# The 64-row score products of two heads (or two maps) by turns into two PSUM banks, in a fixed order on TensorE

## The chip, the cores and the metric

One Trainium2 chip, of which the kernel uses one core. Each engine of the core (TensorE, VectorE, ScalarE, GpSimd, SyncE) takes its instructions in the order in which they stand in the built program, and semaphores tie the engines together. The metric is the device time in microseconds (us) of the whole launch.

## The reference

Three transformer-like blocks one after another on x of 512 tokens by 1024 channels, all in float32. The change touches score products in the first two blocks. Each contracts over 64 channels:

```python
# block 1: 4 heads, 2 maps each, 64 channels per map
sc = jnp.einsum("bhmqd,bhmkd->bhmqk", qb, kt)          # per block of 128 queries
p = jax.nn.softmax(jnp.where(mask, sc, -jnp.inf), axis=-1)
a = p[:, :, 0] - lam * p[:, :, 1]
...
# block 2, gated delta rule: 8 heads of 64 channels
lower = jnp.where(strict, jnp.einsum('bhncd,bhnsd->bhncs', k_beta, k) * decay, 0.0)
attn = jnp.where(causal, jnp.einsum('bhncd,bhnsd->bhncs', q, k) * decay, 0.0)
...
# block 2, rwkv7: 8 heads of 64 channels, token by token
sa = jnp.einsum('bhvk,bhk->bhv', S, a_t)
S = S * w_t[:, :, None, :] + sa[..., None] * b_t[:, :, None, :] + v_t[..., None] * k_t[:, :, None, :]
y_t = jnp.einsum('bhvk,bhk->bhv', S, r_t)
```

The kernel computes both recurrences in chunks of 128 tokens, so that rwkv7 too has score products: of b and k with a (strictly lower part) and of b and k with r.

## The kernel before

The kernel is written in a tile language: the program text says what is computed, tile pools give out buffers, and a scheduler decides when building it in which order each engine's instructions stand. `z.first()` raises the priority of what is inside. What sets the order is therefore text order, priority and the scheduler's own idea of when operands and buffers are ready.

Activations lie with channels on the 128 partitions and 512 tokens along the free side. Two heads, or the two maps of one head, of 64 channels each share a tile: the first on partitions 0 to 63, the second on 64 to 127. A score product of one of them is a matmul with 64 rows (partitions) of contraction; the profile writes it 64\*128. A float32 matmul appears in the trace as two passes, each a weight load and a MATMUL row.

The big projections (`lin`, tiles `mm`, lines L368 to L370) split weights and activations into high and low parts and use three matmuls of 512 columns for each block of 128 channels. Weights come in pieces of eight blocks: a DMA into `wr`, ScalarE makes `wh` (L324), VectorE makes `wl` (L325); each of these has three buffers. Projections that nothing waits for at the moment stand between the small matmuls and fill TensorE.

Block 1, `first`, loop over 4 heads `hd` and 4 query blocks `i`. For each map `m`: a bank of the pool `sc` (two banks) gets the causal mask by a full-array bf16 matmul (L1005, `neg` with the identity `idb`), the diagonal 128 columns of scores on top (L1006, 64 rows), and the `i` earlier blocks of keys (L1008, 64 rows, 128 to 384 columns). Then VectorE takes the row maximum (L1010) and ScalarE the exponential (L1012); the two maps are normalised and combined on VectorE (L1015 to L1018), transposed on TensorE (L1021, `tp`) and multiplied with v (L1025). Elsewhere in VectorE's order stand the 120 taps of a convolution (L750, tiles `cv`).

Block 2, `second`, loop over 4 pairs of heads `j`: `rwkv` (tiles `ra`, `fr`, banks `r`, of which there are three) and `gdn` (tiles `ga`, `fg`, banks `g`, two) run as two interleaved generators, next to the projections of pair `j + 1`. In `rwkv` the helper `scores` makes one head's product: four matmuls of 64 rows by 128 columns into one bank (L1370), then a masked product on VectorE (L1372) that frees the bank. It is called for both heads in turn: `bt` with `at`, `kt` with `at`, and near the end `bt` and `kt` with `rt` (`rb`, `rk`). In `gdn` each head has four matmuls of k with k (L1478) and four of k with q (L1486), each set into a bank of its own. A chain of four such matmuls is eight MATMUL rows.

Of the kernel before, what the change touches and what calls it, by code (L numbers as in the profile page):

```python
# [17 lines left out]
P = 128  # L18
# [167 lines left out]
class K:  # L186
# [65 lines left out]
    def first(self, n=HP):  # L252

        return self.tc.high_priority(offset=n)

    def run(self, *gens):

# [695 lines left out]
def first(z, h):  # L953
    V, A, T = z.V, z.A, z.T
    mult, add, sub = ALU.mult, ALU.add, ALU.subtract
    with z.phase({"aux": 1, "sc": 2, "tp": 1, "o": 1}, qk=12, d=4, p=24, cv=(2, 4 * S), f=6, a=6):
# [5 lines left out]
        ps = f.bank(2)  # L962
# [5 lines left out]
        neg = z.new([P, P], BF16, tag="neg")  # L968
# [6 lines left out]
        qk = []  # L975
# [20 lines left out]
        for hd in range(4):  # L996
            ops = z.bank("o")
            for i in range(4):
                n = (i + 1) * P
                pt, sums = [], ac.small(2)  # L1000
                for m in range(2):
                    ps = z.bank("sc")
                    ql = qk[hd][64 * m:64 * m + 64, i * P:n]
                    kr = qk[4 + hd][64 * m:64 * m + 64]
                    T.matmul(ps[:, i * P:n], lhsT=idb, rhs=neg, start=True, stop=False)  # L1005
                    T.matmul(ps[:, i * P:n], lhsT=ql, rhs=kr[:, i * P:n], start=False, stop=True)  # L1006
                    if i:
                        T.matmul(ps[:, :i * P], lhsT=ql, rhs=kr[:, :i * P], start=True, stop=True)  # L1008
                    mx = ac.small(1)
                    V.tensor_reduce(mx, ps[:, :n], axis=AX.X, op=ALU.max, negate=True)  # L1010
                    pm = ac.t()
                    A.activation(pm[:, :n], ps[:, :n], AF.Exp, bias=mx, accum_out=sums[:, m:m + 1])  # L1012
                    pt.append(pm)
                rs = ac.small(2)
                V.reciprocal(rs, sums)  # L1015
                V.tensor_scalar(rs[:, 1:2], rs[:, 1:2], lam, None, op0=mult)
                V.tensor_scalar(pt[1][:, :n], pt[1][:, :n], rs[:, 1:2], None, op0=mult)
                V.scalar_tensor_tensor(pt[0][:, :n], pt[0][:, :n], rs[:, 0:1], pt[1][:, :n], op0=mult, op1=sub)  # L1018
                tp = z.bank("tp")
                for b in range(i + 1):  # L1020
                    T.transpose(tp[:, b * P:(b + 1) * P], pt[0][:, b * P:(b + 1) * P], z.ident)  # L1021
                at = ac.t()
                A.activation(at[:, :n], tp[:, :n], AF.Copy)
                for b in range(i + 1):
                    T.matmul(ops[:, i * P:n], lhsT=vt[b][:, hd * P:(hd + 1) * P], rhs=at[:, b * P:(b + 1) * P],  # L1025
                             start=b == 0, stop=b == i)
            r = ac.rstd(ac.sumsq([ops]), P)
            o = z.tile("d")
            V.scalar_tensor_tensor(o, ops, z.q("subln"), r, op0=mult, op1=mult)
            V.tensor_scalar(o, o, 1.0 - (0.8 - 0.6), None, op0=mult)  # L1030
            diff.append(o)
# [17 lines left out]
        sc = [], []  # L1049
# [246 lines left out]
    z.V.tensor_tensor_scan(out, mask[p0:p0 + x.shape[0]], x, 0.0, op0=ALU.mult, op1=ALU.add)  # L1296


def rwkv(z, j, rkv, kk, lo, vz, out):

    V, A, T = z.V, z.A, z.T
# [60 lines left out]
    inc = z.k("incl").unsqueeze(1).to_broadcast([P, 4, P])  # L1362
    stm = z.k("strict").unsqueeze(1).to_broadcast([P, 4, P])

    def scores(e, lh, rh, mask):
        ps = c.bank()
        rows = slice(64 * e, 64 * e + 64)
        for i in range(4):
            n = slice(P * i, P * i + P)
            T.matmul(ps[:, n], lhsT=lh[rows, n], rhs=rh[rows, n], start=True, stop=True)  # L1370
        o = c.t()
        V.tensor_tensor(ch(o), ch(ps), mask, op=mult)  # L1372
        return o

    Tt, Lt = [], []
    for e in range(2):
        Lt.append(scores(e, bt, at, stm))
        yield
    inv = [c.invert(x, Tt) for x in Lt]
    for g_ in inv:  # L1380
        next(g_)
    yield
    vtok = vz.rearrange("p c (x n) -> p c x n", n=64)[:, :, 0:4:3]
    c.transposes(v, vtok)
    ak = [ch(scores(e, kt, at, stm)) for e in range(2)]
    yield
    ps = c.bank()
    for i in range(4):
# [16 lines left out]
    for _, ps, x in c.solve(Tt, R, UW):  # L1405
        A.activation(x, ps, AF.Copy)
    yield
    rb = [ch(scores(e, bt, rt, inc)) for e in range(2)]
    rk = [ch(scores(e, kt, rt, inc)) for e in range(2)]
    yield  # L1410

    Y = c.t()
# [40 lines left out]
def gdn(z, j, qkv, gd, tok, out):  # L1453

    V, A, T = z.V, z.A, z.T
    mult, add, sub = ALU.mult, ALU.add, ALU.subtract
    ch = lambda x: x.rearrange("p (c n) -> p c n", c=4)
    c = Chain(z, "ga", "g")
    q, k, v = qkv
    inc = z.k("incl").unsqueeze(1).to_broadcast([P, 4, P])  # L1460
    egb = c.t()
    by = lambda a, hd: tok[:, :, a + hd:a + hd + 1].to_broadcast([P, 4, 64])
    Tt, at, inv = [], [], []
    for e in range(2):
        hd = 2 * j + e
        rows = slice(64 * e, 64 * e + 64)
        gb = c.t()
        z.nc.gpsimd.dma_start(gb, gd[hd].partition_broadcast(P))
        A.activation(egb[rows], gb[rows], AF.Exp)
        V.tensor_tensor(ch(gb), ch(gb), tok[:, :, hd:hd + 1].to_broadcast([P, 4, P]), op=sub)  # L1470
        V.tensor_scalar(gb, gb, 0.0, None, op0=ALU.min)
        A.activation(gb, gb, AF.Exp)
        V.tensor_tensor(ch(gb), ch(gb), inc, op=mult)
        yield
        ps = c.bank()
        for i in range(4):
            n = slice(P * i, P * i + P)
            T.matmul(ps[:, n], lhsT=k[rows, n], rhs=k[rows, n], start=True, stop=True)  # L1478
        l = c.t()
        for i in range(4):  # L1480
            n = slice(P * i, P * i + P)
            V.scalar_tensor_tensor(l[:, n], ps[:, n], tok[:, i, 32 + hd:33 + hd], gb[:, n], op0=mult, op1=mult)
        ps = c.bank()
        for i in range(4):
            n = slice(P * i, P * i + P)
            T.matmul(ps[:, n], lhsT=k[rows, n], rhs=q[rows, n], start=True, stop=True)  # L1486
        V.tensor_tensor(gb, ps, gb, op=mult)
        at.append(ch(gb))
        inv.append(c.invert(l, Tt))
        next(inv[-1])  # L1490
        yield
    ktok = ch(c.transposes(k))
    R, vtok, ke, _ = c.pair()
    c.transposes(v, vtok)
    V.tensor_tensor(q, q, egb, op=mult)
    for e in range(2):
        o = slice(64 * e, 64 * e + 64)
        V.tensor_tensor(ke[:, :, o], ktok[:, :, o], by(64, 2 * j + e), op=mult)
        V.tensor_tensor(ktok[:, :, o], ktok[:, :, o], by(96, 2 * j + e), op=mult)
    yield  # L1500
    while inv:
        for g_ in list(inv):
            if next(g_, z) is z:
                inv.remove(g_)
        yield
    Tt = [ch(x) for x in Tt]

    UW, _, W, U = c.pair()
    for a, ps, x in c.solve(Tt, R, UW):
        for e in range(2):  # L1510
            o = slice(P * e, P * e + P)
            V.tensor_tensor(x[:, :, o], ps[:, :, o], tok[:, 2 * a:2 * a + 2, 32 + 2 * j + e:33 + 2 * j + e].to_broadcast([P, 2, P]),
                            op=mult)
    yield
    Y = c.t()
    for e in range(2):
        ps = c.bank()
        o, x = slice(64 * e, 64 * e + 64), slice(64 - 64 * e, P - 64 * e)
        for i in range(4):
            T.matmul(ps[:, i * P:i * P + P], lhsT=UW[:, i, P * e:P * e + P], rhs=at[e][:, i], start=True, stop=True)  # L1520
        A.activation(Y[o], ps[o], AF.Copy)
        V.tensor_tensor(q[o, P:], q[o, P:], ps[x, P:], op=add)
    yield
    ps = c.bank()
    for i in range(3):
        T.matmul(ps[:, i * P:i * P + P], lhsT=ktok[:, i], rhs=U(i), start=True, stop=True)
    Sv = c.t()
    V.tensor_tensor(ch(Sv)[:, :3], ch(ps)[:, :3], z.bd64.unsqueeze(1).to_broadcast([P, 3, P]), op=mult)
    ps = c.bank()
    for i in range(1, 3):  # L1530
        T.matmul(ps[:, i * P:i * P + P], lhsT=W[:, i], rhs=ktok[:, i], start=True, stop=True)
    Kb = c.t()
    V.tensor_tensor(ch(Kb)[:, 1:3], ch(ps)[:, 1:3], z.bd64.unsqueeze(1).to_broadcast([P, 2, P]), op=mult)
    yield
    for i in (1, 2):
        n, b = slice(i * P, i * P + P), slice(i * P - P, i * P)
        ps = c.bank(P)
        T.matmul(ps, lhsT=Kb[:, n], rhs=Sv[:, b], start=True, stop=True)
        V.scalar_tensor_tensor(Sv[:, n], Sv[:, b], egb[:, i * P + 127:i * P + 128], Sv[:, n], op0=mult, op1=add)
        V.tensor_tensor(Sv[:, n], Sv[:, n], ps, op=add)  # L1540
        yield
    ps = c.bank()
    for i in range(1, 4):
        n = slice(i * P, i * P + P)
        T.matmul(ps[:, n], lhsT=Sv[:, n.start - P:n.start], rhs=q[:, n], start=True, stop=True)
    V.tensor_tensor(Y[:, P:], Y[:, P:], ps[:, P:], op=add)
    yield
    out.append((Y,))
# [570 lines left out]
```

## Time and profile before

| | |
|---|---|
| median of 3 runs | 3328.61 us (3328.02 to 3330.11) |
| the profiled execution's own time | 3330.9 us |
| its span, first to last instruction | 3329.1 us |
| TensorE busy (MATMUL) | 3242.3 us, 97% |
| VectorE busy | 2234.4 us, 67% |
| ScalarE busy | 1497.2 us, 45% |
| mean granted TensorE clock | 0.992 |

A MATMUL row lasts longer than the time after which the next one may start, so that rows overlap and busy time says little about what a matmul costs. What it costs is the time from its start to the start of the next row.

### The profile page before, as it was taken

To read this page: it belongs to the slowest core of one execution; us is meant where nothing else is said; L and a number is where in the kernel's file an instruction comes from. 1 tells how busy PE (TensorE), PEld (TensorE's weight loads), DVE (VectorE), ACT (ScalarE), POOL (GpSimd) and SP (SyncE) were. 2 spreads that over 40 slices of the span, in tenths; PEclk is the share of its full clock that TensorE was granted. 3 is DMA by queue.
4 is the path that set the end of the run, shared out by engine and by line. 5 is a ranking of instruction groups with operands and counts; after the bars stand their busy time and mean duration, and the time that the engine had idled before them with its cause. 6 is when DMAs were issued, how large, how long until landed. Compare 5 with 4: busy or idle time off the path is not lost.

```text
span 3329.1 us, 48326 instructions
## 1 busy us (share of the span) xinstructions
PE 3242.3 (97%) x19041; PEld 2700.3 (81%) x19041; DVE 2234.4 (67%) x3675; ACT 1497.2 (45%) x2491; POOL 101.0 (3%) x186
## 2 busy tenths in 40 slices
PE   7999999999999999999999999999999999999998
PEld 6778888888887887887888887888877778888887
DVE  5696645986578577566887567777687996363344
ACT  6443433432346656654332334645546665232222
POOL 0000000000000000000000000000000001000000
PEclk9999999999999999999999999999999999999999
DMA  4223333665332112125367324222227567423332
GB/s 134 64 70 98 95 117 102 215 202 161 107 103 76 46 50 73 58 64 171 122 203 242 95 81 133 69 78 92 81 80 239 171 208 239 131 88 101 95 95 76
DMA packets 128324, 393.33 MB, mean 118 GB/s; under 512 B 16056, under 2 KB 23480, under 8 KB 128096
## 3 DMA queue, kind: packets, MB, share of 16 engines
q1 hardware_dynamic: 113776, 346.82, 33.6%
q0 software_dynamic: 13168, 42.36, 3.7%
q8 instruction: 150, 2.46, 0.3%
q10 hardware_dynamic: 1152, 1.05, 0.1%
q14 instruction: 78, 0.64, 0.1%
HBM read 358.44 MB, written 31.74 MB: 117 GB/s over the span
## 4 chain that ended last, share of the span: by engine, by line
PE 88%; DVE 6%; ACT 4%; issue 2%; DMA 1%; SPq 0%; POOL 0%; DVEq 0%; ACTq 0%; POOLq 0%
PE mm L368 20%; PE mm L369 20%; PE mm L370 20%; PE mm L354 3%; PE mm L355 3%; PE mm L356 3%; PE s L2082 1%; DVE wl L325 1%; PE s L2068 1%; ACT wh L324 1%; PE r L1370 1%; PE g L655 1%; PE mm L405 1%; PE r L655 1%; PE mm L406 1%
## 5 line engine op out<-in xcount | busy, mean ns | idle before, releaser
L368 PE MATMUL mm<-h,wh 128*128 128x512 f32 x2400 | 947.6, 395 | 1.8 <-ACT t L948 1.5
L369 PE MATMUL mm<-h,wh 128*128 128x512 f32 x2400 | 948.5, 395 | 0.0
L370 PE MATMUL mm<-h,wl 128*128 128x512 f32 x2400 | 947.3, 395 | 0.0
L324 ACT ACTIVATE wh<-wr 128x1024 fp32r<-128x1024 f32 x464 | 491.4, 1061 | 949.8 <-PE mm L369 663.5
L325 DVE TENSOR_TENSOR wl<-wr,wh 128x1024 fp32r<-128x1024 f32 x464 | 567.2, 1224 | 467.6 <-ACT wh L324 462.2
L368 PEld LDWEIGHTS mm<-h,wh 128*128 128x128 f32 x2400 | 452.7, 189 | 98.4 <-issue 5.5
L370 PEld LDWEIGHTS mm<-h,wl 128*128 128x128 f32 x2400 | 452.7, 189 | 96.9 <-issue 6.0
L369 PEld LDWEIGHTS mm<-h,wh 128*128 128x128 f32 x2400 | 452.8, 189 | 96.2 <-issue 5.4
L368 PE MATMUL mm<-p,wh 128*128 128x512 f32 x599 | 233.6, 390 | 0.0
L369 PE MATMUL mm<-p,wh 128*128 128x512 f32 x599 | 233.4, 390 | 0.1
L370 PE MATMUL mm<-p,wl 128*128 128x512 f32 x599 | 233.1, 389 | 0.0
L354 PE MATMUL mm<-h,wh 128*128 128x256 f32 (+1 forms) x480 | 159.5, 344 | 14.4 <-DVE t L1930 5.3
L355 PE MATMUL mm<-h,wh 128*128 128x256 f32 (+1 forms) x480 | 160.1, 339 | 1.1 <-DVE h L569 1.0
L356 PE MATMUL mm<-h,wl 128*128 128x256 f32 (+1 forms) x480 | 158.6, 335 | 0.0
L301 DVE SCALAR_TENSOR_TENSOR ac<-wa,adas,ac 128x1024 f32<-128x1024 f32 x98 | 125.5, 1282 | 23.9 <-DMA wa<-wa 23.5
L369 PEld LDWEIGHTS mm<-p,wh 128*128 128x128 f32 x599 | 112.4, 188 | 23.9 <-DVE p L430 0.8
L368 PEld LDWEIGHTS mm<-p,wh 128*128 128x128 f32 x599 | 112.4, 188 | 23.5
L370 PEld LDWEIGHTS mm<-p,wl 128*128 128x128 f32 x599 | 112.4, 188 | 23.4
L354 PEld LDWEIGHTS mm<-h,wh 128*128 128x128 f32 x480 | 92.4, 198 | 25.8 <-ACT h L568 4.6
L355 PEld LDWEIGHTS mm<-h,wh 128*128 128x128 f32 x480 | 94.3, 198 | 10.0 <-DVE h L569 2.0
L356 PEld LDWEIGHTS mm<-h,wl 128*128 128x128 f32 x480 | 94.6, 198 | 8.5
L750 DVE SCALAR_TENSOR_TENSOR f<-mm,par,f 128x511 f32<-128x511 f32 (+1 forms) x128 | 95.5, 746 | 1.1
(661 smaller groups left out, 5244.6 us busy)
## 6 DMA issues: line engine op xcount, KB each, us to landing
wr<-w SPq DMA_DIRECT2D x464, 512.0 KB, 3.7
wa<-wa SPq DMA_DIRECT2D x96, 512.0 KB, 4.3
e<-cum SPq DMA_DIRECT2D x64, 256.0 KB, 5.1
x<-x POOLq DMA_DIRECT2D x40, 256.0 KB, 4.5
s<-ecum SPq DMA_DIRECT2D x64, 128.0 KB, 4.8
cd<-t POOLq DMA_DIRECT2D x24, 256.0 KB, 2.3
gt<-t POOLq DMA_DIRECT2D x16, 256.0 KB, 2.5
fr<-gt SPq DMA_DIRECT2D x16, 256.0 KB, 3.0
```

Source lines behind the costliest of these rows:

```text
L301: self.V.scalar_tensor_tensor(a, raw, s[:, k, m:m + 1], a, op0=ALU.mult, op1=ALU.add)
L324: self.A.activation(hi, raw, AF.Copy)
L325: self.V.tensor_tensor(lo, raw, hi.bitcast(F32), op=ALU.subtract)
L354: self.T.matmul(ps[:, n], lhsT=wh, rhs=x[0][k][:, n], start=k == 0, stop=False)
L355: self.T.matmul(ps[:, n], lhsT=wh, rhs=x[1][k][:, n], start=False, stop=False)
L356: self.T.matmul(ps[:, n], lhsT=wl, rhs=x[0][k][:, n], start=False, stop=k == last)
L368: self.T.matmul(out, lhsT=wh, rhs=x[0][k], start=k == 0, stop=False)
L369: self.T.matmul(out, lhsT=wh, rhs=x[1][k], start=False, stop=False)
L370: self.T.matmul(out, lhsT=wl, rhs=x[0][k], start=False, stop=k == last)
L405: self.T.matmul(ps, lhsT=a, rhs=wl, start=False, stop=False)
L655: self.z.T.transpose(ps[:, c * P:(c + 1) * P], src[:, c * P:(c + 1) * P], self.z.ident)
L750: z.V.scalar_tensor_tensor(out[:, d:], src[:, :S - d], w[:, n - 1 - d:n - d], out[:, d:], op0=ALU.mult, op1=ALU.add)
```

## The change

The two heads (or maps) get their two banks together, and their matmuls are issued by turns, the second one (partitions 64 to 127) first. `in_order` makes the scheduler keep TensorE's order inside as written; other matmuls may still stand in between. In `gdn` the k with k products of both heads now come after the decay tiles of both heads, then the k with q products of both, then both inversions start. In block 1 the two mask matmuls come first, then the diagonals by turns, then the earlier keys by turns; maxima and exponentials of both maps follow.

```diff
+    def in_order(self):
+        return self.tc.manual_schedule(engines={mybir.EngineType.PE})
...
-                for m in range(2):
-                    ps = z.bank("sc")
-                    ql = qk[hd][64 * m:64 * m + 64, i * P:n]
-                    kr = qk[4 + hd][64 * m:64 * m + 64]
-                    T.matmul(ps[:, i * P:n], lhsT=idb, rhs=neg, start=True, stop=False)
-                    T.matmul(ps[:, i * P:n], lhsT=ql, rhs=kr[:, i * P:n], start=False, stop=True)
-                    if i:
-                        T.matmul(ps[:, :i * P], lhsT=ql, rhs=kr[:, :i * P], start=True, stop=True)
+                two = [z.bank("sc") for _ in range(2)]
+                row = [slice(64 * m, 64 * m + 64) for m in range(2)]
+                q_, k_ = qk[hd], qk[4 + hd]
+                turns = [(row[m], two[m]) for m in (1, 0)]
+                with z.in_order():
+                    for _, ps in turns:
+                        T.matmul(ps[:, i * P:n], lhsT=idb, rhs=neg, start=True, stop=False)
+                    for m, ps in turns:
+                        T.matmul(ps[:, i * P:n], lhsT=q_[m, i * P:n], rhs=k_[m, i * P:n], start=False, stop=True)
+                    for m, ps in turns if i else ():
+                        T.matmul(ps[:, :i * P], lhsT=q_[m, i * P:n], rhs=k_[m, :i * P], start=True, stop=True)
+                for m, ps in enumerate(two):
...
+def halves(z, c, lh, rh):
+    two = [c.bank() for _ in range(2)]
+    with z.in_order():
+        for i in range(4):
+            n = slice(P * i, P * i + P)
+            for e in (1, 0):
+                rows = slice(64 * e, 64 * e + 64)
+                z.T.matmul(two[e][:, n], lhsT=lh[rows, n], rhs=rh[rows, n], start=True, stop=True)
+    return two
...
-    def scores(e, lh, rh, mask):
-        ps = c.bank()
-        rows = slice(64 * e, 64 * e + 64)
-        for i in range(4):
-            n = slice(P * i, P * i + P)
-            T.matmul(ps[:, n], lhsT=lh[rows, n], rhs=rh[rows, n], start=True, stop=True)
-        o = c.t()
-        V.tensor_tensor(ch(o), ch(ps), mask, op=mult)
-        return o
+    def scores(lh, rh, mask):
+        out = []
+        for ps in halves(z, c, lh, rh):
+            o = c.t()
+            V.tensor_tensor(ch(o), ch(ps), mask, op=mult)
+            out.append(o)
+        return out
...
-    rb = [ch(scores(e, bt, rt, inc)) for e in range(2)]
-    rk = [ch(scores(e, kt, rt, inc)) for e in range(2)]
+    rb = [ch(x) for x in scores(bt, rt, inc)]
+    rk = [ch(x) for x in scores(kt, rt, inc)]
...
+        at.append(gb)
         yield
-        ps = c.bank()
-        for i in range(4):
-            n = slice(P * i, P * i + P)
-            T.matmul(ps[:, n], lhsT=k[rows, n], rhs=k[rows, n], start=True, stop=True)
+    for e, ps in enumerate(halves(z, c, k, k)):
         l = c.t()
...
-        ps = c.bank()
-        for i in range(4):
-            n = slice(P * i, P * i + P)
-            T.matmul(ps[:, n], lhsT=k[rows, n], rhs=q[rows, n], start=True, stop=True)
-        V.tensor_tensor(gb, ps, gb, op=mult)
-        at.append(ch(gb))
         inv.append(c.invert(l, Tt))
-        next(inv[-1])
-        yield
+    yield
+    for e, ps in enumerate(halves(z, c, k, q)):
+        V.tensor_tensor(at[e], ps, at[e], op=mult)
+        at[e] = ch(at[e])
+    for g_ in inv:
+        next(g_)
+    yield
```

How this moves TensorE's order shows at three places. A row is one instruction of the built program (a float32 matmul is one row here and two in the trace), `x4` stands for four alike, and the number behind a name is the buffer's. First, block 1, second head, last query block, before; `sc265` and `sc268` are the banks of the two maps:

```order
L1005 MATMUL sc265_1186<-neg82_313,idb83_315 128x128
L1006 MATMUL sc265_1186<-qk139_626,qk102_448 128x128
L1008 MATMUL sc265_1186<-qk139_626,qk102_448 128x384
L369 MATMUL mm396_1724<-h23_119,wh390_1632 128x512
L370 MATMUL mm396_1724<-h22_118,wl391_1633 128x512
L368 MATMUL mm396_1724<-h24_120,wh390_1632 128x512
L1005 LDWEIGHTS idb83_315
L1005 MATMUL sc268_1194<-neg82_313,idb83_315 128x128
L1006 MATMUL sc268_1194<-qk139_626,qk102_448 128x128
L1008 MATMUL sc268_1194<-qk139_626,qk102_448 128x384
```

The same place of TensorE's order in the changed kernel (its line numbers are larger by a few: L1011, L1013 and L1015 are L1005, L1006 and L1008 of before, and L372 to L374 are L368 to L370); of the seven projection rows after the first mask matmul the last three are shown:

```order
L1011 MATMUL sc266_1208<-neg82_313,idb83_315 128x128
...
L372 MATMUL mm392_1741<-h30_126,wh386_1649 128x512
L373 MATMUL mm392_1741<-h31_127,wh386_1649 128x512
L374 MATMUL mm392_1741<-h30_126,wl387_1650 128x512
L1011 LDWEIGHTS idb83_315
L1011 MATMUL sc265_1207<-neg82_313,idb83_315 128x128
L1013 MATMUL sc266_1208<-qk139_626,qk102_448 128x128
L1013 MATMUL sc265_1207<-qk139_626,qk102_448 128x128
L1015 MATMUL sc266_1208<-qk139_626,qk102_448 128x384
L1015 MATMUL sc265_1207<-qk139_626,qk102_448 128x384
```

The first mask matmul stands some projections ahead, and the four 64-row matmuls of the two maps stand next to each other, one map after the other. Second, block 2, first pair of heads, TensorE's order at `rb` and `rk` before (two heads of `rb`, then two of `rk`, and the first use of them at L1418):

```order
L1370 MATMUL r1658_8960<-fr1417_7999,ra1470_8280 128x128 x4
L1370 MATMUL r1660_8967<-fr1417_7999,ra1470_8280 128x128 x4
L1370 MATMUL r1662_8974<-fr1417_7999,fr1422_8033 128x128 x4
L1370 MATMUL r1664_8981<-fr1417_7999,fr1422_8033 128x128 x4
L1418 MATMUL r1667_8989<-ra1659_8965,cra1654_8942 128x128
```

And after, from the last two rows of `rb` on (L1315 is the line of `halves`, L1559 is L1545 of before, a product of `gdn`, and L1435 is L1418 of before):

```order
L1315 MATMUL r1658_9016<-fr1417_8047,ra1470_8328 128x128
L1315 MATMUL r1657_9015<-fr1417_8047,ra1470_8328 128x128
L1315 MATMUL r1662_9033<-fr1417_8047,fr1422_8081 128x128
L1559 MATMUL g1665_9049<-fg1432_8149,ga1649_8987 128x128 x3
L1315 MATMUL r1661_9032<-fr1417_8047,fr1422_8081 128x128
L1315 MATMUL r1662_9033<-fr1417_8047,fr1422_8081 128x128
...
L1315 MATMUL r1661_9032<-fr1417_8047,fr1422_8081 128x128
L1435 MATMUL r1667_9055<-ra1659_9028,cra1653_8998 128x128
```

The eight matmuls of `rb` stand by turns without a break; of `rk` one matmul stands alone, then three others, then the remaining seven by turns. Third, block 2, first pair of heads, the k with q products of `gdn` after the change (before, each head's four stood right behind its four of k with k):

```order
L373 MATMUL mm1703_9244<-h893_4737,wh1695_9179 128x512
L1315 MATMUL g1493_8407<-fg1432_8149,fg1438_8188 128x128
L374 MATMUL mm1703_9244<-h892_4736,wl1696_9180 128x512
...
L374 MATMUL mm1703_9244<-h900_4744,wl1696_9180 128x512
L1315 MATMUL g1492_8406<-fg1432_8149,fg1438_8188 128x128
L1315 MATMUL g1493_8407<-fg1432_8149,fg1438_8188 128x128
L1315 MATMUL g1492_8406<-fg1432_8149,fg1438_8188 128x128
```

Here too one matmul stands alone, 13 projection matmuls follow, and then the other seven by turns. ScalarE's order in block 2 changes as well: it holds 28 loads of activation tables instead of 26, two more at the border from the first to the second pair of heads and from the third to the fourth, two fewer at the border between. TensorE's order from block 3 on is the same as before.

## Rows read from the trace of the kernel before

**Rows 1.** The chain of work that ended last, shares of the span by engine.

```profile
PE 88%; DVE 6%; ACT 4%; issue 2%; DMA 1%; SPq 0%; POOL 0%; DVEq 0%; ACTq 0%; POOLq 0%
```

**Rows 2.** Windows: length, busy us of PE, PEld, DVE, ACT, POOL; clock; DMA.

```profile
95.00:130.00 35.00, 35.00 (x192) 27.13 (x191) 16.77 (x34) 15.12 (x34) 0.00 (x0) 1.00 0.22 62
130.00:256.00 126.00, 125.50 (x588) 93.73 (x587) 113.74 (x202) 59.40 (x111) 0.00 (x0) 1.00 0.22 67
```

**Rows 3.** The same view, block 2: first pair of heads, border to the second.

```profile
1020.00:1131.00 111.00, 110.27 (x763) 96.30 (x762) 82.14 (x163) 66.40 (x134) 1.08 (x2) 1.00 0.13 41
1131.00:1158.00 27.00, 24.69 (x98) 18.54 (x97) 12.64 (x18) 19.66 (x26) 2.17 (x4) 0.94 0.38 118
```

**Rows 4.** TensorE in order of time: start, length, row; rwkv's rb, rk.

```profile
1115.15 1.38 PE L1370 MATMUL r<-fr,ra 64*128 64x128 f32 x13
...
1116.48 0.27 PE L1370 MATMUL r<-fr,fr 64*128 64x128 f32 x1
1116.48 0.27 PE L1370 MATMUL r<-fr,ra 64*128 64x128 f32 x1
1116.59 0.27 PE L1370 MATMUL r<-fr,fr 64*128 64x128 f32 x1
...
1118.18 0.49 PE L1418 MATMUL r<-ra,cra 128*128 128x128 f32 x2
```

**Rows 5.** The same view: 64-column halves of the array by turns, block 3.

```profile
2545.50 1.74 PE L2082 MATMUL s<-e,g 128*64 128x128 f32 x26
2547.17 0.49 PE L370 MATMUL mm<-h,wl 128*128 128x512 f32 x1
```

**Rows 6.** The same view: attention, query blocks 0 and 3, one map each.

```profile
204.06 0.23 PE L1005 MATMUL sc<-neg,idb 128*128 128x128 bf16 x1
204.22 0.48 PE L1006 MATMUL sc<-qk,qk 64*128 64x128 f32 x2
204.64 0.50 PE L369 MATMUL mm<-h,wh 128*128 128x512 f32 x1
204.97 0.39 PE L370 MATMUL mm<-h,wl 128*128 128x512 f32 x1
205.20 0.40 PE L368 MATMUL mm<-h,wh 128*128 128x512 f32 x1
...
233.14 0.23 PE L1005 MATMUL sc<-neg,idb 128*128 128x128 bf16 x1
...
234.36 0.50 PE L368 MATMUL mm<-h,wh 128*128 128x512 f32 x1
```

**Rows 7.** One line's matmuls: count, least, median and greatest ns.

```profile
L1006 PE MATMUL sc<-qk,qk x64: 272/322/373, 100.3 to 233.5; 64*128 64x128 f32 x64
...
L1370 PE MATMUL r<-ra,ra x64: 272/272/373, 1044.6 to 1430.6; 64*128 64x128 f32 x64
```

**Rows 8.** What VectorE waited for, 130 to 256 us: total, times, longest.

```profile
DVE wl L325 <- ACT wh L324: 6.6, 9, 1.8
```

**Rows 9.** TensorE in order of time: gdn's and rwkv's chains.

```profile
1038.81 1.16 PE L1478 MATMUL g<-fg 64*128 64x128 f32 x8
1040.79 0.50 PE L369 MATMUL mm<-h,wh 128*128 128x512 f32 x1
...
1044.64 1.71 PE L1370 MATMUL r<-ra,ra 64*128 64x128 f32 x16
1046.28 0.50 PE L370 MATMUL mm<-h,wl 128*128 128x512 f32 x1
...
1194.41 1.16 PE L1370 MATMUL r<-ra,ra 64*128 64x128 f32 x8
1195.50 0.50 PE L370 MATMUL mm<-h,wl 128*128 128x512 f32 x1
```

**Rows 10.** VectorE in order of time: the products of two heads of rk.

```profile
1118.15 1.28 DVE L1372 TENSOR_TENSOR ra<-r,con 128x512 f32<-128x512 f32 x2
```

**Rows 11.** ScalarE in order of time: one load of activation tables.

```profile
1138.51 1.28 ACT L608 ACT_TABLE_LOAD   x1
```

More of the change, by code (lines that the diff above doesn't have):

```diff
@@ L1363, in rwkv @@
     stm = z.k("strict").unsqueeze(1).to_broadcast([P, 4, P])
-    def scores(e, lh, rh, mask):
-        ps = c.bank()
-        rows = slice(64 * e, 64 * e + 64)
-        for i in range(4):
-            n = slice(P * i, P * i + P)
-            T.matmul(ps[:, n], lhsT=lh[rows, n], rhs=rh[rows, n], start=True, stop=True)
-        o = c.t()
-        V.tensor_tensor(ch(o), ch(ps), mask, op=mult)
-        return o
-    Tt, Lt = [], []
-    for e in range(2):
-        Lt.append(scores(e, bt, at, stm))
-        yield
+    def scores(lh, rh, mask):
[5 more added lines that the diff above has]
+        return out
+    Tt, Lt = [], scores(bt, at, stm)
+    yield
     inv = [c.invert(x, Tt) for x in Lt]
@@ L1384, in rwkv @@
     c.transposes(v, vtok)
-    ak = [ch(scores(e, kt, at, stm)) for e in range(2)]
+    ak = [ch(x) for x in scores(kt, at, stm)]
     yield
@@ L1481, in gdn @@
             n = slice(P * i, P * i + P)
-            V.scalar_tensor_tensor(l[:, n], ps[:, n], tok[:, i, 32 + hd:33 + hd], gb[:, n], op0=mult, op1=mult)
-        ps = c.bank()
-        for i in range(4):
-            n = slice(P * i, P * i + P)
-            T.matmul(ps[:, n], lhsT=k[rows, n], rhs=q[rows, n], start=True, stop=True)
-        V.tensor_tensor(gb, ps, gb, op=mult)
-        at.append(ch(gb))
-        inv.append(c.invert(l, Tt))
-        next(inv[-1])
-        yield
+            V.scalar_tensor_tensor(l[:, n], ps[:, n], tok[:, i, 32 + 2 * j + e:33 + 2 * j + e], at[e][:, n], op0=mult, op1=mult)
+        inv.append(c.invert(l, Tt))
+    yield
[4 more added lines that the diff above has]
+        next(g_)
+    yield
     ktok = ch(c.transposes(k))
```

## The prediction

> **What bounds the kernel now.** I read the chain of waits first: 88% of the span is TensorE, so time taken from TensorE shortens the kernel as long as nobody else becomes late [rows 1]. Then the windows of the two stages that the change touches. In block 1's attention TensorE is busy without a gap, but so, nearly, is VectorE: from 130 to 256 us it works 113.7 of 126 us, while in the 35 us before it has only 16.8 us of work [rows 2]. In block 2 TensorE is busy for 110.3 of 111 us while a pair of heads is computed and VectorE for 82.1; at the border to the next pair, 27 us long, TensorE has 2.3 us of gaps [rows 3]. Last the order of time on TensorE, for prices: what counts there is the distance from one start to the next, not the length of a row.
>
> **Do two halves of the array run at the same time?** Everything hangs on this, and the trace already answers it. In rwkv's `rb` and `rk` the scheduler has put the chain of head 0 and that of head 1 one behind the other, and where they meet, two passes of different heads start at the same time, 1116.48, and again 0.11 us later, the step at which one chain alone goes [rows 4]. Two chains of different halves cost 1.64 us together, two of the same half (`gdn`, one head) 1.98 [rows 9]. So before the change neighbouring chains already overlap, but only at their ends. Where block 3 takes the two column halves by turns, 26 passes take 1.67 us, 0.06 each instead of 0.11 [rows 5]. I take it that row halves by turns pair as fully.
>
> **Attention in block 1.** One map of one query block costs 0.58 us for block 0 (204.06 to 204.64) and 1.22 for block 3 (233.14 to 234.36) [rows 6]; the two between lie evenly, so four blocks cost 3.6 us, and 8 maps 28.8. There are 64 passes on the diagonals, 4 for each of 16 pairs of maps [rows 7]. By turns a pair costs one map and one more mask matmul: 14.4 us saved, less 16 mask matmuls. Alone such a matmul fills 0.16 us up to the next start, but that holds the change from full to half array; at the other end the change shows as 0.33 us for a projection pass whose neighbour takes 0.23, so 0.10. A mask matmul beside another full one is thus bounded by 0.16 and by a quarter of 0.23 (a quarter of the columns), 0.06; I take 0.06, since the change then happens once: 1.0 us. In 11 of the 16 pairs the two maps had projections between them, and one change back of 0.10 goes: 1.1. Together 14.4 - 1.0 + 1.1 = 14.5 us less TensorE time, a quarter of it for each head.
>
> VectorE does not let all of that through. Its work (maxima, normalising, 120 taps, splitting of weights) is unchanged, and in the order after as many taps stand ahead of the last head's end as before. Head 0 lies mostly where VectorE has room, and I count its 3.6 us whole. Heads 1 to 3 would save 10.9 us in a stretch where VectorE is idle for only 12.3. Of that, 6.6 us is `wl` waiting for `wh`, which waits for a buffer that TensorE frees: this shrinks when TensorE is faster [rows 8]. The other 5.7 are waits for a result just asked for, and I let them stand. So heads 1 to 3 give 6.6, at least 0 (if none of it shrinks) and at most 10.9. Attention: 10.2 us.
>
> On evacuation the Trainium skill, TensorEngine Tiling (Array Packing), section PSUM Bottleneck, says that tiling speeds up TensorE but not the emptying of PSUM, which may become the limit. By that rule alone heads 1 to 3 give nothing more once VectorE is full; by the rows VectorE has 6.6 us to give. This is the first rival below.
>
> **gdn.** Sixteen chains now: twelve stand two together at 1.98 us, six times; four stand alone at 1.09 [rows 9]: 16.3 us, plus eleven changes back at 0.10 (one chain is cut in two): 17.4. After: four pairs of k with k undivided, each as one chain and a change, 1.19; four pairs of k with q of which one matmul stands alone ahead, 0.42 (204.22 to 204.64 [rows 6]) and 0.10 for its change, then the rest at 1.19: 1.71. Together 11.6, so 5.8 us less. The wait for the banks that VectorE must empty lies behind the projections between; if these ran out, its two rows of products (0.64 us each [rows 10]) would be exposed four times, 5 us.
>
> **rwkv.** `bt` and `kt` with `at`: fourteen chains in seven pairs of 1.64, two alone at 1.09 (one cut in two, 0.2 more), ten changes back: 14.9 us. After: three pairs whole at 1.19, five divided at up to 1.71: 12.1; 2.8 less. `rb` and `rk`: 3.02 us for four chains now (1115.15 to 1118.18) [rows 4]. After: 1.09 for `rb`, 0.22 for the first of `rk`, two changes of 0.10 around three moved matmuls, 1.09 for the rest: 2.5, so 0.5 less, four times. But `rk`'s next matmul needs a bank of `rb`, which VectorE frees by a product of 0.64 us [rows 10] that now starts only when the whole pair is done; three moved matmuls cover about that. Bounds: 0 to 2.0; I take 1.2, nearer the upper end because of that cover. rwkv: 4.0.
>
> **ScalarE.** Two more table loads of 1.28 us [rows 11], at borders where ScalarE is busy for 19.7 of 27 us [rows 3] and which the chain follows: net 2.6 us lost if all is exposed. Bounds: 0 (TensorE has projections to do) and 5.1 (the two fewer at the middle border save nothing). I take 2.6.
>
> **Sum.** 10.2 + 5.8 + 4.0 - 2.6 = 17.4 us. The profiled execution took 3330.9 us, so 3313.5; the median of the runs is 2.3 us below that execution: **3311.2 us**.
>
> **Rivals.**
> 1. *VectorE takes over in attention*, and the table loads are all exposed: only head 0 gains, 3.6, block 2 gives 9.8 - 5.1, together 8.3 us: 3320.3. For it: 12.3 us of idle time against 10.9 wanted. Against: half of that idle time is waiting for TensorE.
> 2. *The turns don't pair*, because the two passes of one float32 matmul stay together and the next half waits for both. Then TensorE loses the overlap at the ends of rwkv's chains, 12 pairs by 0.34 (1.98 - 1.64) or less, 4 us, and gains the eleven changes, 1.1: 3331, no difference that a measurement can tell. Against: 1116.48.
> 3. *Slower: a pair waits for both its banks.* TensorE's order is fixed, so at each of the 40 pairs (16 and 24) everything behind, projections too, stands if one bank isn't free. VectorE and ScalarE get both results at once and empty them one after the other. At 0.5 us of standing for each pair the 20.0 us of the first three terms are gone; from 0.7 us on (28 us, with 2.6 of table loads) the kernel is over 0.2% slower, 3339. For it: two banks in `sc` and `g`, one matmul of many pairs alone ahead. Against: in all but a few places projections stand between a bank's emptying and its next use.
> 4. *All is let through*: 14.5 + 5.8 + 4.8 and no exposed loads, 25 us: 3303.5.
>
> **How the numbers follow.** Chances: the forecast, with gains from 11 to 22 us, 0.56; rival 1, 0.20; rival 2, 0.08; rival 3, 0.06; rival 4, 0.10. What a measurement of this kernel can tell from no change is about 0.2%, 6.7 us. Faster by more: the forecast, rival 4 and most of rival 1, 0.83; within: the rest of rival 1 and most of rival 2, 0.11; slower: 0.06. The range reaches from rival 4 with a little more, 3301, to rival 1 with 3 us of further waits, 3323; outside it lie rivals 2 and 3 and some of the ends, not quite 2 in 10.
>
> **What the profile after would show.** In TensorE's order of time, passes of the halves starting two at a time, a whole pair of chains in about 1.1 us instead of 1.64 to 1.98, and a pair of maps in 0.6 to 1.3 us. From 130 us to the end of the fourth head, VectorE busy over 95%, with `wl` waiting less. In block 2 no new waits of TensorE for `r` and `g` banks over 0.5 us. Two more table loads on ScalarE. The prediction is wrong if the starts of a pair lie 0.11 us apart one by one, if TensorE has gaps in attention behind VectorE, or if borders in block 2 have grown by more than the table loads.

## The result, and the profile after

The changed kernel takes 3309.55 us in the median of six runs (3308.21 to 3314.44); the kernel before, run beside it, 3328.48 (3326.53 to 3330.94). Ratio 0.9945, 95% interval 0.9933 to 0.9958: 18.9 us faster. The profiled execution took 3309.3 us, 21.6 less than that of before; the profiles thus show some 3 us more than the medians do, and a part of it is TensorE's clock (below).

The head of the page of after: TensorE is busy with MATMULs for 24.6 us less, the work of VectorE is nearly the same (2232.0 us against 2234.4).

```profile
span 3307.5 us, 48313 instructions
PE 3217.7 (97%) x19041; PEld 2671.8 (81%) x19041; DVE 2232.0 (67%) x3675; ACT 1496.2 (45%) x2493; POOL 101.5 (3%) x186
```

**The halves pair.** TensorE's order of time at the first k with k products of `gdn` (start, length, line, form, count):

```profile
1012.18 1.16 PE L1315 MATMUL g<-fg 64*128 64x128 f32 x16 [0.69 <-DVE fg L1238]
1013.27 0.50 PE L373 MATMUL mm<-h,wh 128*128 128x512 f32 x1
```

Sixteen passes of two heads take 1.09 us up to the next start, as long as one head's eight took before; two chains of one half took 1.98 [rows 9]. And one pair of maps of the last head's last query block:

```profile
214.66 0.22 PE L1011 MATMUL sc<-neg,idb 128*128 128x128 bf16 x1
214.68 0.47 PE L373 MATMUL mm<-h,wh 128*128 128x512 f32 x1
215.00 0.39 PE L374 MATMUL mm<-h,wl 128*128 128x512 f32 x1
215.22 0.40 PE L372 MATMUL mm<-h,wh 128*128 128x512 f32 x1
...
215.92 0.23 PE L1011 MATMUL sc<-neg,idb 128*128 128x128 bf16 x1
216.08 0.49 PE L1013 MATMUL sc<-qk,qk 64*128 64x128 f32 x4
216.41 0.81 PE L1015 MATMUL sc<-qk,qk 64*128 64x384 f32 x4
217.15 0.50 PE L372 MATMUL mm<-h,wh 128*128 128x512 f32 x1
```

From the second mask to the next projection 1.23 us for both maps; before, 1.22 for one [rows 6]. The first mask, alone at 214.66, seems to cost 0.02, but the projection behind it takes 0.32 instead of 0.22 to 0.24.

**The sums.** All of these are added up from the trace's rows. The distance from each row's start to the next one on TensorE, added over all rows of a kind: attention's masks and scores (144 rows) 28.75 us before and 15.36 after; `gdn`'s score chains (128 rows) 16.82 and 10.37; `rwkv`'s (256 rows) 25.93 and 21.91. In `rwkv`'s 21.91 are 1.5 us of waits: at three places of `bt` with `at` the row that follows isn't ready, and the last pass is followed 0.51, 0.77 and 0.78 us later instead of the usual 0.20; without them it is 20.4. In experiments 1 and 5, whose block 2 is that of before, `gdn` has 16.4 instead of 16.8. Counting TensorE's MATMULs from the start and comparing the times of equal numbers, after is ahead by 0.4 us at 90 us, by 11.0 from 300 us (attention is done) to 940, by 20.4 behind block 2, by 21.6 at the end.

**Attention**, the windows of [rows 2] again (columns: us, PE, PEld, DVE, ACT, POOL busy, PEclk, DMA), then TensorE's waits from 95 to 300 us, then VectorE's wait of [rows 8], 130 to 256:

```profile
95.00:130.00 35.00, 34.88 (x209) 26.31 (x208) 18.84 (x41) 18.48 (x39) 0.00 (x0) 1.00 0.20 62
130.00:256.00 126.00, 124.47 (x619) 95.15 (x618) 120.36 (x209) 61.03 (x110) 0.00 (x0) 1.00 0.25 75
```

```profile
PE sc L1011 <- ACT a L1020: 1.5, 2, 0.8
PE mm L373 <- DVE p L434: 1.1, 1, 1.1
```

```profile
DVE wl L329 <- ACT wh L328: 0.2, 1, 0.2
```

VectorE is now busy for 95.5% of the stretch; `wl` no longer waits (6.6 us before); TensorE has waits of 2.6 us in all, where before it had one of 0.5.

**Block 2.** TensorE's waits from 950 to 1525 us:

```profile
PE r L620 <- ACT ra L1297: 5.3, 3, 4.1
PE g L659 <- ACT ga L1206: 3.9, 1, 3.9
PE g L1315 <- DVE fg L1238: 1.9, 3, 0.7
PE mm L372 <- ACT ra L433: 1.9, 1, 1.9
PE g L659 <- DVE ga L692: 1.0, 2, 0.5
```

The 3.9 us at the start of block 2 stand in both kernels. New is the wait of 4.1 us for a copy of ScalarE (L1297, the split of a sum's operand) at the first border between pairs; before, the longest of its kind was 1.1. Two large waits of before have shrunk to 1.9 us each:

```profile
PE g L1478 <- DVE fg L1230: 3.2, 3, 1.3
PE mm L368 <- ACT ra L429: 3.2, 1, 3.2
```

In sum TensorE hardly stands still for longer. Here is the same stretch of work, block 2 with a little around it, before, in experiment 1 (which has block 2 as before) and after (same columns as above; what the busy time of PE leaves of the stretch is idle):

```profile
940.00:1560.00 620.00, 602.98 (x3770) 511.75 (x3770) 440.46 (x831) 364.45 (x669) 18.96 (x35) 0.98 0.24 73
929.00:1546.00 617.00, 598.78 (x3774) 508.40 (x3774) 440.60 (x831) 364.67 (x669) 18.96 (x35) 0.99 0.23 73
929.00:1540.00 611.00, 592.47 (x3772) 493.93 (x3772) 439.56 (x831) 365.61 (x671) 19.46 (x35) 0.99 0.24 73
```

Idle are 17.0, 18.2 and 18.5 us: the new wait took the place of others. What stands in front of that copy on ScalarE:

```profile
1130.39 0.62 ACT L628 ACTIVATE ra<-ra 128x512 f32<-128x512 f32 x1
1130.91 0.68 ACT L1166 ACTIVATE fr<-mm,omu 128x512 f32<-128x512 f32 x1
1131.48 1.05 ACT L328 ACTIVATE wh<-wr 128x1024 fp32r<-128x1024 f32 x1
1132.55 1.28 ACT L612 ACT_TABLE_LOAD   x1
1133.84 1.06 ACT L612 ACTIVATE cga<-cga 128x1024 f32<-128x1024 f32 x1
1134.80 0.61 ACT L1297 ACTIVATE ra<-ra 128x512 fp32r<-128x512 f32 x1
```

Its operand is the square of 1130.39, done by 1131.01; it starts at 1134.80, behind a mixing copy, a weight piece, a table load and an exponential.

**The clock.** In block 2 some projection passes start 0.43 us apart instead of 0.227, at the lower of TensorE's two levels (1.2 GHz), in the stretches behind its waits at the borders (granted clock 0.89 from 1140 to 1160 us before, 0.87 from 1120 to 1140 after). That cost 5.9 us in the profiled execution of before, 4.5 in that of after and 2.3 in the first experiment's. So 1.4 us of the profiled difference are clock, and executions of one program can differ by more.

### The profile page after: what moved, and what is told of

The parts are those of the page before. It is cut to its first block, busy times and chain, and to the rows that moved or that the text cites. A ratio compares the mean times of both kernels' runs of the same rounds, so it can differ in the third digit from the quotient of the medians.

```text
span 3307.5 us, 48313 instructions
## 1 busy us (share of the span) xinstructions
PE 3217.7 (97%) x19041; PEld 2671.8 (81%) x19041; DVE 2232.0 (67%) x3675; ACT 1496.2 (45%) x2493; POOL 101.5 (3%) x186
## 5 line engine op out<-in xcount | busy, mean ns | idle before, releaser
L372 PE MATMUL mm<-h,wh 128*128 128x512 f32 x2400 | 945.7, 394 | 1.6 <-ACT t L952 1.5
L374 PE MATMUL mm<-h,wl 128*128 128x512 f32 x2400 | 947.2, 395 | 0.0
L372 PEld LDWEIGHTS mm<-h,wh 128*128 128x128 f32 x2400 | 452.4, 188 | 98.1 <-issue 6.0
L374 PEld LDWEIGHTS mm<-h,wl 128*128 128x128 f32 x2400 | 452.1, 188 | 96.4 <-issue 4.5
L372 PE MATMUL mm<-p,wh 128*128 128x512 f32 x599 | 233.6, 390 | 0.0
L374 PE MATMUL mm<-p,wl 128*128 128x512 f32 x599 | 233.0, 389 | 0.0
L372 PEld LDWEIGHTS mm<-p,wh 128*128 128x128 f32 x599 | 112.4, 188 | 23.4
L374 PEld LDWEIGHTS mm<-p,wl 128*128 128x128 f32 x599 | 112.4, 188 | 23.4
```

The source lines that it names most:

```text
L372: self.T.matmul(out, lhsT=wh, rhs=x[0][k], start=k == 0, stop=False)
L374: self.T.matmul(out, lhsT=wl, rhs=x[0][k], start=False, stop=k == last)
```

## Experiments

Each was timed beside the kernel before; the medians of before in the three groups were 3328.0, 3327.4 and 3328.0 us.

**1. Only attention changed** (block 2 as before).

> Only block 1's attention is changed; block 2 is that of the kernel before. The theory (halves by turns run at the same time, and the parts of the change add up): by the end of block 1 TensorE is 11.0 us ahead of the kernel before, as in the changed kernel, and nothing more comes after that: 3328.5 - 11.0 = 3317.5 us, ratio 0.9967. The rival (block 2's gain seen in the profile is partly a difference in granted clock between two executions, so that block 2 as before may also come out some us faster by chance): 3313 to 3316 in the profiled execution, with the clock rows at the borders of block 2 not the same as before. A third case (attention's gain needs block 2's new order): 3328.

3316.06 us, ratio 0.9961 (0.9949 to 0.9974). Over attention TensorE gains 10.6 us, and the runs show no loss of them later: 12.0 by medians. The profile shows 4 us more behind that, in a block 2 that is unchanged; 3.6 us of it are the passes at the low clock (2.3 instead of 5.9). The rival named the right thing for the single profile; for the change the parts count as measured.

**2. Only block 2 changed.**

> Only block 2 (gdn and rwkv) is changed; attention is that of the kernel before. If the parts add up, 18.9 - 11.0 = 7.9 us less than the kernel before: 3320.6 us, ratio 0.9976; score chains on TensorE 32.3 us instead of 42.8. If about 4 of the 9.5 us that the profiles show for block 2 come from TensorE's granted clock alone and not from the change: 3323 to 3325. If the longer wait for ScalarE at the first border (4.1 us instead of 1.1) belongs to the change, it shows again here.

3322.45 us, ratio 0.9982 (0.9973 to 0.9991): 5.6 us. With experiment 1 (12.0) that makes 17.5 of the 18.9. The score chains cost 32.3 us as in the changed kernel, 10.5 less than before, so about half of that saving comes through. TensorE waits for the copy at the first border as long as in the changed kernel: that wait belongs to the change.

**3. One half after the other.** All else as changed.

```diff
-        for i in range(4):
-            for e in (1, 0):
+        for e in (1, 0):
+            for i in range(4):
```

(in attention likewise: diagonal and earlier keys of one map, then of the other)

> Everything as in the changed kernel (two banks asked for together, fixed order, gdn's new order, the masks first), but not by turns: all matmuls of the second half, then all of the first. The theory (the gain is the two row halves running at the same time): a pair of chains costs 1.64 to 2.0 us again instead of 1.09 and a pair of maps of block 3 2.2 instead of 1.23, so that some 24 us of TensorE time come back, less 24 + 16 overlaps of 0.3 us at the seams (12): 3309.5 + 12 to 24 = 3322 to 3333 us, ratio 0.998 to 1.002. The rival (the gain is the new grouping: fewer changes between the full and the half array, the masks together, both banks at once): 3310 to 3314 us.

3318.76 us, ratio 0.9971 (0.9960 to 0.9983), between the two: each was right in one block. The same two places as above, in this kernel:

```profile
1012.92 1.68 PE L1315 MATMUL g<-fg 64*128 64x128 f32 x16 [0.70 <-DVE fg L1238]
1014.53 0.50 PE L373 MATMUL mm<-h,wh 128*128 128x512 f32 x1
...
216.04 0.50 PE L1013 MATMUL sc<-qk,qk 64*128 64x128 f32 x4
216.37 0.82 PE L1015 MATMUL sc<-qk,qk 64*128 64x384 f32 x4
217.12 0.50 PE L372 MATMUL mm<-h,wh 128*128 128x512 f32 x1
```

The pair of `gdn` costs 1.61 us instead of 1.09, and block 2's chains 42.8 in sum, as before the change. But the pair of maps costs 1.08, as by turns, and TensorE gains 10.5 us over attention. A map has up to four passes, a chain of block 2 eight. So two groups of four passes overlap fully when they stand next to each other, two of eight only at the seam.

**4. No fixed order.** `in_order` does nothing.

> The changed kernel without the fixed order: the scheduler may separate the turns. In the built program gdn's k with q and some of rk then stand four and four, and in attention the mask, diagonal and earlier keys of one map stand ahead of the other's, while bt with at and kt with at mostly stay by turns. The theory (only matmuls that stand by turns run together): 16 pairs of maps lose the pairing except at the seam, some 9 us, and block 2 loses 4 to 8 pairs of 0.5 us, 3 us: 3319 to 3323 us, ratio 0.997. The rival (TensorE pairs whatever stands near, the order is of no account): 3309.5 us.

3326.66 us, ratio 0.9996 (0.9987 to 1.0005): next to nothing is left. In attention:

```profile
223.75 0.23 PE L1011 MATMUL sc<-neg,idb 128*128 128x128 bf16 x1
223.91 0.48 PE L1013 MATMUL sc<-qk,qk 64*128 64x128 f32 x2
224.24 0.81 PE L1015 MATMUL sc<-qk,qk 64*128 64x384 f32 x2
224.97 0.50 PE L373 MATMUL mm<-h,wh 128*128 128x512 f32 x1
```

One map alone costs 1.22 us again; masks and scores add up to 28.0. In block 2 the chains cost 36.6, a saving of 6.2, of which TensorE's lead over before keeps 4.3 behind block 2; from 90 us on it grows by 3.0 in all. Both expectations missed. A full-array mask or projection between the maps is enough to part them: at 108.83 and 110.04 us of this trace two maps stand with only the second one's mask between them, and cost 1.21 and 1.23 us.

**5 and 6. Sixty taps less**, in the kernel before and in the changed one.

```diff
-            conv(z, o, th, w, 31)
+            conv(z, o, th, w, 16)
```

> The kernel before with 60 of the convolution's 120 taps in block 1 left out, some 45 us of VectorE work out of the stretch in which attention runs; TensorE's work is unchanged. TensorE has next to no gaps there, so no time should come off: 3328 us, within 2. It is the base for the next kernel.

> The changed kernel with the same 60 taps left out. In the changed kernel TensorE spends 13.4 us less on attention's masks and scores, but is only 11.0 us ahead at the end of block 1, and has waits there for a bank of scores that ScalarE's exponential must free (1.5 us) and for a tile split on VectorE (1.1 us). The theory (those 2.4 us are lost because VectorE is full): here TensorE is 13 to 14 us ahead of the base with the taps left out by the end of block 1, and the two waits are gone. The rival (VectorE is not the reason; two results in two banks are emptied one after the other whatever else VectorE has to do): 11.0 to 11.9 again and the wait for the bank stays.

3329.07 us (1.0004, 0.9995 to 1.0013) and 3308.55 (0.9946, 0.9934 to 0.9958). Counted from their lead at 89 us, TensorE gains 12.0 us over attention with the taps out, 10.6 with them in. Its waits there in experiment 6:

```profile
PE sc L1011 <- ACT a L1020: 0.8, 2, 0.5
```

The wait for the split tile is gone and that for the bank halved: 1.4 us were lost to a full VectorE. The gain is not the 13 to 14 expected, so the saving itself was counted too high.

**7. Two by two.** Block 2 with two matmuls of one half, then two of the other.

```diff
-            for e in (1, 0):
+        for i, e in [(i, e) for h in (0, 2) for e in (1, 0) for i in (h, h + 1)]:
```

> The changed kernel, but in block 2 two matmuls (four passes) of one half and two of the other by turns, instead of one and one. Four by four, the chains of block 2 cost 42.8 us in all, by turns 32.3, while in attention, where a map has two matmuls, one map after the other cost as little as by turns (12.3 us and 12.2). The theory (TensorE starts passes of the other half some three passes ahead, so groups of four passes pair nearly in full): 32 to 35 us for block 2's chains, and 3306 to 3312 us in all; the built program also has two table loads less on ScalarE (65 instead of 67), which if the wait of 4.1 us at the first border is theirs takes 3 us off: 3306.5. The rival (only passes that stand side by side pair, one at each seam): 39 to 40 us and 3316 us.

The first pair of `gdn`, and the largest wait of block 2:

```profile
1013.33 1.23 PE L1314 MATMUL g<-fg 64*128 64x128 f32 x16 [0.69 <-DVE fg L1238]
1014.50 0.50 PE L373 MATMUL mm<-h,wh 128*128 128x512 f32 x1
```

```profile
PE r L620 <- ACT ra L1297: 7.8, 3, 3.9
```

Block 2's chains cost 33.1 us, as the theory said (1.17 for this pair). Yet the kernel takes 3313.47 us (0.9958, 0.9946 to 0.9971), not the 3306 to 3312 expected and by medians 3.9 us more than the changed one, though the intervals of the two ratios overlap. With two table loads less it waits longer for the copy, 7.8 us instead of 5.3, so the number of table loads is not what sets this wait.

**8 and 9. The split ahead.** The changed kernel, and the kernel before, with

```diff
-        part(self.z, hi, lo, x)
+        with self.z.first():
+            part(self.z, hi, lo, x)
```

> The changed kernel, with the priority raised for the two instructions (copy on ScalarE, subtraction on VectorE) that split the operand of a sum over channels. At the first border of block 2 TensorE stands 4.1 us for such a copy, which in ScalarE's order stands behind a copy, a table load and an exponential although its operand is ready; in this kernel's order it stands ahead of them. The theory (of the 10.5 us that TensorE saves in block 2, 4 or so are lost again at the borders, because ScalarE's order puts other work ahead of what TensorE waits for): the waits for the copy shrink from 5.3 us to under 2, and 3309.5 - 3.5 = 3306 us. The rival (the loss is elsewhere, and a wait that goes here comes back in the next stage): 3309 to 3311 us.

> The kernel before with the same raised priority, to tell what this order is worth without the change. Before, TensorE waits 2.2 us in all for these copies. The theory (the 4.1 us belong to the order that the change brought about): no more than 2 us off, 3326 to 3328 us, and the changed kernel with it is further below this one than the 18.9 us of the change alone. The rival (the raised priority helps any kernel of this kind as much): 3324 us.

On top of the change 3305.47 us, ratio 0.9930 (0.9918 to 0.9943); on the kernel before 3330.25 (1.0009, 1.0000 to 1.0018). ScalarE at the first border, in experiment 8:

```profile
1126.81 0.62 ACT L629 ACTIVATE ra<-ra 128x512 f32<-128x512 f32 x1
1127.33 0.61 ACT L1490 ACTIVATE ga<-ga 128x512 f32<-128x512 f32 x1
1127.85 0.61 ACT L1298 ACTIVATE ra<-ra 128x512 fp32r<-128x512 f32 x1
```

and TensorE's three largest waits of block 2, in experiment 8 and then in 9:

```profile
PE g L660 <- ACT ga L1207: 3.9, 1, 3.9
PE r L621 <- ACT ra L1298: 3.2, 4, 1.2
PE r L1344 <- ACT cga L609: 2.2, 2, 1.8
```

```profile
PE mm L368 <- ACT ra L429: 4.3, 1, 4.3
PE g L656 <- ACT ga L1199: 3.9, 1, 3.9
PE r L617 <- ACT ra L1290: 3.8, 2, 2.6
```

The copy follows its square by 0.4 us instead of 3.8, with as many table loads as in the changed kernel. The waits for these copies fall from 5.3 us to 3.2, not to under 2 as expected; others fall too, and all of TensorE's waits in block 2 add up to 10.0 us instead of 14.4. The kernel is 4.1 us faster than the changed one by medians of different groups (the intervals of the two ratios overlap a little). The priority was raised for every split of this kind, so how much the one copy at the first border is worth by itself isn't shown. Before the change the same priority gives nothing: the waits for these copies grow from 2.2 to 3.8 us there, and that of L368 from 3.2 to 4.3. This is the fastest version measured.

## Why the prediction held, and where not

The forecast was 3311.2 us, and 3309.55 was measured. Its terms (us; the measured ones from the sums and runs above):

| step | forecast | measured |
|---|---|---|
| attention, saved on TensorE | 14.5 | 12.0 to 12.5 |
| attention, let through | 10.2 | 10.6 (12.0 by the runs of experiment 1) |
| gdn | 5.8 | 6.0 to 6.5 |
| rwkv | 4.0 | 4.0: 5.5 on the passes, less 1.5 of waits |
| borders of block 2 | -2.6 | TensorE idle 0.3 to 1.5 longer |
| block 2, let through | 7.2 | 5.6 (experiment 2) to 6.5 (changed kernel against experiment 1) |
| sum | 17.4 | 18.9 by medians, 17.5 by experiments 1 and 2 |

The mechanism was right and the sum came close, but the closeness is in part luck: in attention 2 us too much saving and 2 to 3 us too much loss cancel, and in block 2 the loss is larger than forecast and has other reasons. The terms of `gdn` and `rwkv` hold changes between full and half array as well, the measured ones passes alone. Two sums are also slightly off as added up: `gdn`'s chains of before are 16.2 and not 16.3, and `rb` with `rk` after are 2.6 and not 2.5, so that their upper bound is 1.7 and not 2.0.

*Pairing.* Right: starts two at a time, 1.09 us for a pair. That turns are what makes attention gain was wrong by experiment 3: there standing side by side is enough, and the fixed order that keeps masks and projections out is worth the whole gain (experiment 4). In block 2 the turns are worth 9.2 us (experiment 3 against the changed kernel, by medians).

*Attention's saving* was 2 us too high, and the step that failed is the lone mask matmul, taken at 0.06 us, the lower bound. In experiments 5 and 6 masks and scores fall by 13.3 us, but the projections between them rise by 1.1, of which 0.3 is more waiting. By their distances a lone mask takes 0.04 to the next start, the projection behind it 0.09 more, that ahead of it 0.05 more: some 0.17, just over the upper bound of 0.16. It stands alone in 15 of the 16 pairs, which makes 1.7 us more. The changes back are there, and more than eleven: 26 projections behind scores cost 2.9 us more than others in the one, 13 cost 1.4 more in the other, 0.11 each.

*What VectorE lets through.* Head 0's 3.6 us came nearly whole: counted by equal numbers of MATMULs, after is 3.6 us further ahead at 123 us than at 90, 3.1 at 125. At 251 us it is 11.3, and 0.7 are given back by 298, at the wait for the split tile (1.1 us at 259). That wait is one of the prediction's own signs of being wrong, a gap behind VectorE in attention; it showed, but small. The sentence "The other 5.7 are waits for a result just asked for" came out: VectorE is idle for 5.6 of 126 us. That 4.3 us of a saving of 14.5 are lost was too much; of 12.0 to 12.5 only 1.4 to 1.9 are, the 1.4 shown by experiments 5 and 6 to be VectorE's. The Trainium skill, TensorEngine Tiling (Array Packing), section PSUM Bottleneck, warns that emptying PSUM may become the limit once TensorE is faster (it speaks of four times faster). The traces agree on the place and make it small: 2.6 us of waits, of which 1.5 for a bank.

*gdn and rwkv.* The passes were priced rightly. Without the changes back the prediction's own sums give 16.2 us before and 10.4 after for `gdn` and 25.8 and 20.4 for `rwkv`; measured are 16.4 to 16.8 and 10.4, and 25.9 and 20.4 without waits. That 4.0 came out for `rwkv` as forecast is luck: the waits of 1.5 us are not those that the prediction allowed for between `rb` and `rk`. They lie at `bt` with `at`, where transposes of `gdn` stand next and wait for what VectorE or ScalarE hands them.

*ScalarE and the borders.* The reason was wrong. The profile does have two more table loads (2493 instructions on ScalarE, 2491 before), but experiment 7 has none more and waits longer, experiment 8 has them and waits less. What the new order of instructions brought about is one wait of 4.1 us at the first border, for a copy that stands late in ScalarE's order; as other waits shrank, TensorE's idle time in block 2 grew by 0.3 to 1.5 us only. "In block 2 no new waits of TensorE for `r` and `g` banks over 0.5 us" failed there, though the wait is for what goes into the bank and not for the bank.

*Where the rest of block 2's saving went.* The chains save 10.1 to 10.5 us, 5.6 to 6.5 come through. Idle time is not the main reason. Other rows became dearer: in the changed kernel and in experiments 2 and 6 the 256 products of 64 by 64 take 18.8 us instead of the 17.7 of the three traces with the old block 2, and 20 to 22 projections are 0.36 to 0.40 us from the next start where 3 to 5 were. A part belongs to the new order and not to the turns: experiment 3 has the new order with chains as dear as before, and is 2.7 us slower than experiment 1 by medians of one group, though their intervals overlap. The shares of the single rows stay open.

*Rival 3*, a pair waiting for both banks, showed in attention as the bank's 1.5 us, two waits in 16 pairs, far from its 0.5 us at each of 40. Rivals 1 and 4 lie on either side of what happened. Open is also why the scheduler puts the copy where it does.

## What to carry to other kernels

Matmuls that use different row halves of TensorE run together when few passes stand between them: group them by at most four passes a half (eight lose most of it; five to seven were not tried), and above all let no full-array matmul come between, which here needed a fixed order. Price a small matmul by what its neighbours become, not by its own row. When an engine on the path gets faster, look next at the order of the engine that feeds it at stage borders: putting the splits ahead there was worth 4 us by medians, and nothing before the change.

## What was not expected of the hardware

- By the trace's start times TensorE starts passes of the other half ahead of earlier ones, so the order of the program is not quite the order of starts. The kernel before shows it with names: the first pass of `rk` (`fr,fr`) stands behind all of `rb` (`fr,ra`) in TensorE's order, and starts at 1116.26, before three passes of `rb`, which start at 1116.37, 1116.48 and 1116.59 [rows 4]:

```profile
1116.26 0.37 PE L1370 MATMUL r<-fr,fr 64*128 64x128 f32 x1
1116.37 0.27 PE L1370 MATMUL r<-fr,ra 64*128 64x128 f32 x1
```

  In experiment 3 the pair of `gdn` has starts at 1012.92, 1013.10, .21, .32, .44, .55, .66 and .77 (the chain issued first) and 1013.44, .65, .77, .88 and on to 1014.32 (the chain issued second; which is which is read from the steps of 0.11 us): here too the second chain starts with three passes of the first still to come. The Trainium skill, TensorE: Matmul & The Clock Gate, section The mechanism, says of such tiles that weight loads are pulled ahead and that MATMULs start in program order; the first fits (the second chain's first weight load starts at 1013.44, too), the second does not fit these rows.
- The reach is short: groups of eight passes overlap by 0.37 us (1.98 to 1.61), groups of four nearly wholly (1.17, by turns 1.09).
- A full-array matmul of 128 bf16 columns, alone among float32 projections, costs 0.17 us with what its neighbours lose, though its own row is followed 0.02 to 0.04 us later.
